# Transposes of an attention step in one block, scores two steps ahead, v in shared 8-row units

## Chip, core and metric

The kernel runs on one core of a Trainium2 chip. The metric is the time of one execution in device microseconds; the median of three executions stands for a kernel. All loads, the matmuls, the softmax and the stores are in that time. Engines are named as in the profile: PE (matmul; PEld its weight loads), DVE, ACT, POOL, and SP, which here issues the DMA transfers.

## What is computed

An encoder layer over two sequences, a prompt of 256 tokens and a sample of 2048 tokens, width 1024. Tokens stand on a grid of 64 columns: 4 rows for the prompt, 32 for the sample. One half of the inner width (8 heads of 64) is neighbourhood attention: a query sees 8 rows by 16 columns of keys. The other half is a Fourier mix. The part that matters here, from the reference:

```
def one_row(r):
    rs = jnp.clip(r - kr // 2, 0, rows - kr)
    ...
    k_slab = lax.dynamic_slice_in_dim(kg, rs, kr, axis=1)[:, :, slab_cols]
    v_slab = lax.dynamic_slice_in_dim(vg, rs, kr, axis=1)[:, :, slab_cols]
    logits = jnp.einsum('bjqhd,bijkhd->bhjqik', q_blk, k_slab).astype(jnp.float32) * scale
    ...
    logits = jnp.where(valid[:, :, None, :], logits + bias, NEG_INF)
    p = jax.nn.softmax(logits.reshape(shp[:4] + (kr * K_SLAB_COLS,)), axis=-1).reshape(shp)
    out = jnp.einsum('bhjqik,bijkhd->bjqhd', p.astype(v.dtype), v_slab)
...
mixed = jnp.concatenate([rms_norm(y_a, g_na) * jax.nn.silu(z_a),
                         rms_norm(y_f, g_f) * jax.nn.silu(z_f)], axis=-1)
out = mixed @ w_out
return x + rms_norm(out, g_post)
```

## The kernel before

The program has three stages: the input projections (to about 540 us), the Fourier mix (to 611 us), then attention together with the Fourier half of the output projection (611 to 855 us), and last the attention half of the output projection.

**Groups and steps.** Attention works through 36 groups `G`: 4 pairs of heads `pr`, and 9 groups `i` for each. Group `i` = 0 is the prompt (`R` None). The others are a set of rows `R` = 0 to 3 and a half `hc` of the columns; `HALF[R]` names the first of two runs of 4 query rows. Runs are the partitions 0 to 63 and 64 to 127 of a tile ("halves" `y`). A group has two column blocks `b` (widths `w` of 24 or 32 key columns) and two heads `h`. For `R` over 0 the two halves see 11 key rows each, starting 4 rows apart; for `R` = 0 it is 8 rows each.

**One step** of the loop over `k` (from line 1549) does `scores` of `G[k]`, transposes and second matmul of the group before, `G[k-1]`, and one half of a tile of the Fourier output projection. PE's order is written out by hand and is the order of the program:

- `scores(G[k])` (L1169): 64x64 matmuls into four PSUM banks, two passes for each f32 matmul. `bias_max` (L1191, DVE) adds the bias table and takes the row maximum, `exps` (L1196, ACT) exponentiates with a sum, `soft` (L1200 DVE reciprocal, L1203 POOL) divides.
- `transp(f, 0)` (L1470): transposes of the weights `w` of block 0, 64 rows each; half 0 goes to bank `ptb[0]`, half 1 to `ptb[1]`. ACT copies the one, DVE the other, to `pt` (L1473).
- `f_mm(k, range(6))` (L1413): the first 6 of 12 matmuls of 128x128 with 512 columns into a bank with tag "b".
- `transp(f, 1)`: the same for block 1, into the same two banks.
- `f_mm(k, range(6, 12))`, then `f_evac(k)`: DVE (even `k`, L1445) or ACT (odd `k`, L1442) takes the bank out.
- `pv(f)` (L1486): weights times v into the one bank with tag "c"; DVE multiplies by the gate `za` (L1506), ACT squares it (L1512, or L1508 for `pr` = 0), POOL adds the squares up (L1513).

A few steps also hold `f_norm` or `a_norm` (L1450, L1457: sums of squares by matmuls of one column), `ys_mul` and `ys_split` (the inputs of later `f_mm`), and in steps 2 to 7 the squares `YSQ` (L1601, L1602). After the loop come the attention tiles `a_mm`.

**PSUM** has eight banks: three "a" and two "b", two "t" (`ptb`), one "c". Three of the four score banks of a step come from "a" and the fourth from "b".

**v.** `prep_v` (L1134) loads for each group its own 4 chunks of 4 key rows for both blocks, in 4 DMAs; 3 buffers, issued at the end of step `k` for `G[k+1]`. Chunks start at row `4R'` of half 0; half 1 stands in the score tile with its key rows rotated (`ORD`), so that two of its three chunks lie at the same place as those of half 0. `pv` thus has four products per block and head: two for both halves (128 columns), one for each half alone (64 columns).

Of the kernel before, what the change touches and what calls it, by code (L numbers as in the profile page):

```python
# [178 lines left out]
def build(tc, A, O):  # L179
# [934 lines left out]


    def prep_v(g):
        cs = slice(g["pr"] * 128, g["pr"] * 128 + 128)
        v = g["v"] = jl.tile([128, 8, 128], F32, tag="v", name="v", bufs=VB)
        g["za"] = jl.tile([128, 256], F32, tag="za", name="za", bufs=VB)
        g["ch"], g["pp"] = [], []  # L1120
        if g["R"] is None:
            nc.sync.dma_start(v[:, :4], vP.rearrange("k r c e -> (r c) k e")[:, :, cs])
            nc.sync.dma_start(g["za"], zD[1, cs, :TP])
            for b in range(2):
                g["ch"].append([(0, 128)])
                g["pp"].append([(0, x, 128, 2 * b + x, True, True) for x in range(2)])
            return
        r0, r1 = HALF[g["R"]]
        for b, w in enumerate(g["kw"]):
            n = 4 * w  # L1130
            src = vD[2 * g["hc"] + b]
            parts = ((0, 3, r0 - 4), (3, 1, r1 + 3)) if g["R"] else ((0, 2, 0), (2, 2, 24))
            for j, m, r in parts:
                nc.sync.dma_start(v[:n, 4 * b + j:4 * b + j + m],  # L1134
                                  src[r:r + 4 * m].rearrange("r c e -> (r c) e")[:, cs]
                                  .rearrange("(j p) e -> p j e", p=n))
            if g["R"]:
                g["ch"].append([(0, n), (n, n), (2 * n, 3 * w)])
                g["pp"].append([(1, None, n, 4 * b + 1, True, False), (2, None, 3 * w, 4 * b + 2, False, False),
                                (0, 0, n, 4 * b, False, False), (0, 1, n, 4 * b + 3, False, True)])  # L1140
            else:
                g["ch"].append([(0, n), (n, n)])
                g["pp"].append([(j, x, n, 4 * b + 2 * x + j, j == 0, j == 1) for x in range(2) for j in range(2)])
        for x, n, r in halves(g):
            t0 = TP + 1024 * (r // 16) + 512 * g["hc"] + 32 * (r % 16)
            nc.sync.dma_start(g["za"][:, x:x + n], zD[1, cs, t0:t0 + n])


    def scores(g):
        nr = g["nr"]  # L1150
        kk = KK[g["pr"]].rearrange("p (r c) -> p r c", c=64)
        if "w" in g:
            sp = [ps.tile([128, 352], F32, tag="c", name="s", bufs=1), *ptb,
                  ps.tile([128, 352], F32, tag="a", name="s", bufs=3)]
        else:
            sp = [ps.tile([128, 352], F32, tag="b" if x == 3 else "a", name="s", bufs=2 if x == 3 else 3)
                  for x in range(4)]
        R = g["R"]
        for b, w in enumerate(g["kw"]):
            if R is None:  # L1160
                seq = [(y, 0, 4, 0, KP0[2 * b + y]) for y in range(2)]
            else:
                c0, r = KC0[2 * g["hc"] + b], 4 + HALF[R][0] - 4 * (R > 0)
                seq = [(0, r, 11, 0, c0), (1, r + 11, 4, 0, c0), (1, r + 4, 7, 4, c0)] if R else \
                    [(y, r + 24 * y, 8, 0, c0) for y in range(2)]
            for y, k, n, j, c0 in seq:
                for h in range(2):
                    hs = slice(64 * h, 64 * h + 64)
                    nc.tensor.matmul(sp[2 * b + h][64 * y:64 * y + 64, j * w:(j + n) * w],  # L1169
                                     g["q"][hs, 128 * b + 64 * y:128 * b + 64 * y + 64],  # L1170
                                     kk[hs, k:k + n, c0:c0 + w], start=True, stop=True)
# [250 lines left out]

    def f_mm(k, js=range(12)):
        d, n = ftiles[k // 2], k % 2
        if js[0] == 0:
            d["p"] = ps.tile([128, 512], F32, tag="b", name="po", bufs=2)
        out_mm(d, n, js, d["p"], lambda n, x, c: wo1[n][c][:, x])

    def a_mm(d, n, js=range(12)):
        if js[0] == 0:  # L1430
            d["p"] = ps.tile([128, 512], F32, tag="a" if n else "b", name="po", bufs=3 if n else 2)
        out_mm(d, n, js, d["p"], lambda n, x, c: WO[x][:, c, n * 512:n * 512 + 512])

# [13 lines left out]
    def f_norm(ts):  # L1447
        p = ps.tile([128, 18], F32, tag="c", name="pfn", bufs=1)
        for t in ts:
# [4 lines left out]
    def a_norm(ds):  # L1454
        p = ps.tile([128, 128], F32, tag="c", name="pna", bufs=1)
        for j, d in enumerate(ds):
# [3 lines left out]

    def transp(g, b):
        ch = g["ch"][b]
        n, z = len(ch) * 128, ch[0][1]
        o = jp.tile([128, 2, 384], F32, tag="pt", name="pt", bufs=PB)
        m = len(ch)
        for h in range(2):
            for j, (c0, nk) in enumerate(ch):
                for y in range(2):
                    ys, x = slice(64 * y, 64 * y + 64), 64 * (h * m + j)
                    nc.tensor.transpose(ptb[y][:nk, x:x + 64], g["w"][b][ys, h, c0:c0 + nk], ident[ys, ys])  # L1470
        ov = o.rearrange("p h (j y x) -> p y h j x", y=2, x=64)
        for y, copy in ((0, nc.scalar.copy), (1, V.tensor_copy)):
            copy(ov[:z, y, :, :m], ptb[y][:z, :n].rearrange("p (h j x) -> p h j x", h=2, x=64))  # L1473
        g["pt"] = g.get("pt", []) + [o]

    yt = {}

    def pv(g):
        pr, R = g["pr"], g["R"]
        p = ps.tile([128, 2, 128], F32, tag="c", name="pv", bufs=1)  # L1480
        for b, pp in enumerate(g["pp"]):
            for j, y, nk, v, first, last in pp:
                o = slice(0, 128) if y is None else slice(64 * y, 64 * y + 64)
                for h in range(2):
                    hs = slice(64 * h, 64 * h + 64)
                    nc.tensor.matmul(p[hs, b, o], g["v"][:nk, v, hs], g["pt"][b][:nk, h, j * 128 + o.start:j * 128 + o.stop],  # L1486
                                     start=first, stop=last)
# [44 lines left out]
    f_mm(0)  # L1532
    transp(G[0], 0)
    f_norm(range(2))
    transp(G[0], 1)
    ys_mul(ftiles[1])
    soft(G[1], 1)
    run_later()
# [3 lines left out]
    f_evac(1)  # L1542
    pv(G[0])
    ys_load(ftiles[2])
    prep_v(G[2])
    prep(G[4])
    for k in range(2, len(G) + 1):
        pr, i = divmod(k, 9)
        g, f = G[k] if k < len(G) else None, G[k - 1] if k else None
        if pr < 3:  # L1550
# [11 lines left out]
        if 24 <= k < 32:  # L1562
            y = k - 24
            nc.sync.dma_start(WO[y % 2][:, y // 2].bitcast(F32), woD[0, y % 2, y // 2])
        x = k // 2 + 1
        if g:
            scores(g)
            if 2 < k < 34 and k % 2 == 0:
                ys_mul(ftiles[x])
                if x + 1 < 18:  # L1570
                    ys_load(ftiles[x + 1])
            bias_max(g, 0, 0)
            exps(g, 0, 0)
            bias_max(g, 0, 1)
            bias_max(g, 1, 0)
        if f:
            transp(f, 0)
        if g:
            exps(g, 0, 1)
            bias_max(g, 1, 1)  # L1580
            exps(g, 1, 0)
            f_mm(k, range(6))
            soft(g, 0)
            exps(g, 1, 1)
            if k in NT:
                f_norm(NT[k])
            if k in (32, 34):
                a_norm(atiles[:6] if k == 32 else atiles[6:10])
# [5 lines left out]
        if g:  # L1594
            soft(g, 1)
            if k == 2:
                ys_mul(ftiles[x])
                ys_load(ftiles[x + 1])
# [4 lines left out]
        if g:  # L1603
            f_mm(k, range(6, 12))
        else:
            a_mm(atiles[0], 0, range(6, 12))
        if pr < 3 and i == 8:
            mask_p(pr + 1)
# [12 lines left out]
        if k + 3 < len(G):  # L1621
            prep(G[k + 3])
        if k == 28:
# [21 lines left out]
    def a_evac(d, n):  # L1645
        if n == 0:
            d["sa"] = sm.tile([128, 6], F32, tag="sa", name="sa")
        evac(d, d.pop("p"), slice(n * 512, n * 512 + 512), n)

# [52 lines left out]
    for j, d in enumerate(atiles):  # L1702
# [25 lines left out]
        a_mm(d, 1)  # L1728
        a_evac(d, 1)
# [20 lines left out]
```

## Time and profile before

| | |
|---|---|
| three executions | 960.94, 959.48, 960.78 us; median 960.78 |
| the profiled execution | 960.85 us, its span 959.1 us (1.75 us lie around the span) |
| PE busy, 618 to 848 us (the step loop) | 228.09 of 230.00 us |
| DVE, ACT, POOL busy there | 140.34, 137.40, 118.33 us |
| DMA share there | 0.89 at 266 GB/s |

How it is read: a busy PE only says that a matmul is under way; matmuls overlap, and a block of them that starts late because the array had to empty still counts as busy. So the time of a block is taken from its start to the start of the next block, in the timeline. In a timeline row stand the start and the duration in us, engine, line, operation, tile written and tiles read, shape, the count, and in brackets the idle time before it with its releaser. "64*96 64x64" is 64 rows by 96 columns of weights with 64 rows by 64 columns streamed past.

### The profile page before, as it was taken

What the parts mean: (1) busy time and instruction counts of PE and PEld (TensorE: products, weight loads), DVE (VectorE), ACT (ScalarE), POOL (GpSimd) and SP (SyncE); (2) the same over time, 40 slices, a digit from 0 to 9 for tenths busy, and PEclk for the clock granted to TensorE, in tenths of its full rate; (3) what the DMA queues carried; (4) which work ended last, traced back from release to release, by engine and by line L of the source; (5) the groups of instructions that cost most, each with busy time, mean ns of one, the idle gap of its engine ahead of it and who ended that gap; (6) DMA issues with size and microseconds to landing.
All of it is one profiled execution on the core that took longest, in us unless ns stands there. A gap on an engine that the chain in (4) does not pass through costs nothing.

```text
span 959.1 us, 18563 instructions
## 1 busy us (share of the span) xinstructions
PE 947.5 (99%) x6608; PEld 780.6 (81%) x6608; DVE 667.1 (70%) x1303; ACT 468.7 (49%) x1035; POOL 339.8 (35%) x338
## 2 busy tenths in 40 slices
PE   9999999999999999999999999999999999999996
PEld 7889988888888888888888888877777776888885
DVE  6387978777866976776767354676655655559997
ACT  6846676523333632223444144666555655644443
POOL 3101202445730401533433000554456554424444
PEclk9999999999999999999999999999999999999998
DMA  9899686558746998489989788598898899899993
GB/s 335 320 378 363 206 310 242 171 215 294 276 191 256 368 411 315 178 271 318 324 281 322 262 304 319 206 255 249 266 279 270 242 282 295 256 325 336 335 347 116
DMA packets 158363, 270.67 MB, mean 282 GB/s; under 512 B 22656, under 2 KB 98304, under 8 KB 155392
## 3 DMA queue, kind: packets, MB, share of 16 engines
q1 hardware_dynamic: 158128, 269.50, 81.4%
q8 instruction: 52, 0.85, 0.3%
q14 instruction: 39, 0.32, 0.1%
q10 hardware_dynamic: 144, 0.00, 0.0%
HBM read 180.91 MB, written 95.88 MB: 289 GB/s over the span
## 4 chain that ended last, share of the span: by engine, by line
PE 96%; DMA 2%; DVE 1%; ACT 1%; issue 0%; DVEq 0%; SPq 0%; ACTq 0%
PE po L1413 21%; PE mm L175 18%; PE mm L176 18%; PE mm L174 18%; PE pv L1486 5%; PE s L1169 4%; PE ptb L1470 3%; PE pab L1014 2%; PE py L174 1%; PE py L176 1%; PE py L175 1%; DMA oD<-ofs 1%; DMA rv<-wv 0%; PE ppq L1051 0%; PE pz L175 0%
## 5 line engine op out<-in xcount | busy, mean ns | idle before, releaser
L174 PE MATMUL mm<-xh,wa 128*128 128x512 f32 x448 | 174.4, 389 | 0.0
L175 PE MATMUL mm<-xl,wa 128*128 128x512 f32 x448 | 174.3, 389 | 0.0
L176 PE MATMUL mm<-xh,wa 128*128 128x512 f32 x448 | 174.3, 389 | 0.0
L176 PEld LDWEIGHTS mm<-xh,wa 128*128 128x128 f32 x448 | 84.1, 188 | 17.5
L174 PEld LDWEIGHTS mm<-xh,wa 128*128 128x128 f32 x448 | 84.1, 188 | 17.5
L175 PEld LDWEIGHTS mm<-xl,wa 128*128 128x128 f32 x448 | 84.1, 188 | 17.2
L1203 POOL TENSOR_SCALAR w<-w,m 128x352 f32<-128x352 f32 (+4 forms) x136 | 75.3, 567 | 55.9 <-DVE m L1200 49.7
L1413 PE MATMUL po<-wo,yh 128*128 128x512 f32 x272 | 92.0, 419 | 0.0
L551 POOL TENSOR_TENSOR ws<-wr 128x512 f32<-128x512 f32 x16 | 21.5, 1341 | 185.1 <-DMA wr<-wz 128.2
L1413 PE MATMUL po<-w,yh 128*128 128x512 f32 x280 | 86.8, 391 | 0.0
L566 DVE TENSOR_TENSOR wa<-wr,wa 128x512 fp32r<-128x512 f32 x60 | 57.1, 959 | 33.2 <-ACT wa L565 32.9
L1196 ACT ACTIVATE w<-w,m 128x352 f32<-128x352 f32 (+4 forms) x136 | 70.2, 519 | 13.2 <-DVE m L1191 12.9
L868 DVE TENSOR_TENSOR f<-u,mm 128x512 f32<-128x512 f32 x64 | 43.6, 681 | 33.6 <-PE mm L176 28.8
L175 PE MATMUL mm<-vl,xh 128*128 128x512 f32 x168 | 65.5, 390 | 0.2 <-DVE vl L497 0.2
L176 PE MATMUL mm<-vh,xl 128*128 128x512 f32 x168 | 65.4, 389 | 0.0
L174 PE MATMUL mm<-vh,xh 128*128 128x512 f32 x168 | 65.4, 389 | 0.0
L1413 PEld LDWEIGHTS po<-w,yh 128*128 128x128 f32 x280 | 52.3, 188 | 10.8
L1191 DVE CUSTOM_DVE_ANT_1 w<-s,tb 128x264 f32<-128x264 f32 (+3 forms) x124 | 51.8, 454 | 11.1 <-PE s L1169 10.3
L565 ACT CAST wa<-wr 128x512 fp32r<-128x512 f32 x60 | 36.3, 617 | 45.0 <-PE mm L176 17.6
L1486 PEld LDWEIGHTS pv<-pt,v 96*64 96x64 f32 (+2 forms) x1088 | 45.0, 137 | 14.7 <-issue 11.7
L1413 PEld LDWEIGHTS po<-wo,yh 128*128 128x128 f32 x272 | 45.8, 188 | 11.4
L1413 PE MATMUL po<-w,yl 128*128 128x512 f32 x140 | 54.5, 389 | 0.0
(245 smaller groups left out, 2187.1 us busy)
## 6 DMA issues: line engine op xcount, KB each, us to landing
wr<-wz SPq DMA_DIRECT2D x48, 512.0 KB
vl<-sD SPq DMA_DIRECT2D x20, 512.0 KB
xm<-xm SPq DMA_DIRECT2D x9, 1024.0 KB
oD<-ofs SPq DMA_DIRECT2D x18, 512.0 KB
of<-oD SPq DMA_DIRECT2D x18, 512.0 KB
yr<-yD SPq DMA_DIRECT2D x34, 256.0 KB
zD<-f SPq DMA_DIRECT2D x16, 512.0 KB
woD<-wo SPq DMA_DIRECT2D x16, 512.0 KB
```

The source lines that it names most:

```text
L174: nc.tensor.matmul(out, lh, rh, start=first, stop=False)
L175: nc.tensor.matmul(out, lh, rl, start=False, stop=False)
L176: nc.tensor.matmul(out, ll, rh, start=False, stop=last)
L565: nc.scalar.copy(o[:, 0], src)
L566: nc.vector.tensor_tensor(out=o[:, 1], in0=src, in1=o[:, 0].bitcast(F32), op=ALU.subtract)
L868: nc.vector.tensor_tensor(out=dst(f, b), in0=src(uu[u]), in1=src(p), op=op)
L1169: nc.tensor.matmul(sp[2 * b + h][64 * y:64 * y + 64, j * w:(j + n) * w], g["q"][hs, 128 * b + 64 * y:128 * b + 64 * y + 64], kk[hs, k:k + ...
L1191: nc.vector.tensor_tensor_reduce(out=rows(g["w"][b][:, h, :n], w), in0=rows(g["s"][2 * b + h][:, :n], w), in1=tv, scale=1.0, scalar=3.0e38 ...
L1196: nc.scalar.activation(w, w, AF.Exp, bias=m[:, h:h + 1], scale=-1.0, accum_out=m[:, 2 + h:3 + h])
L1203: nc.gpsimd.tensor_scalar(w, w, m[:, 4 + h:5 + h], 1.0, ALU.mult, ALU.mult)
L1413: nc.tensor.matmul(p, (d["l"] if x == 2 else d["h"])[:, c], w(n, int(x == 1), c), start=j == 0, stop=j == 11)
L1486: nc.tensor.matmul(p[hs, b, o], g["v"][:nk, v, hs], g["pt"][b][:nk, h, j * 128 + o.start:j * 128 + o.stop], start=first, stop=last)
```

## The change

The transposes of both blocks of a group now run as one block of `transp(g)` into four banks, and `f_mm` as one block of 12. The group transposed and multiplied in step `k` is `G[k-2]`; the loop has one step more. The order on PE becomes transposes, scores, `f_mm`, (norms), `pv`. The two "b" banks become `ptb[2]` and `ptb[3]`: block 1's transposes write there first, and later in the same step `f_mm(k)` writes into one of them, `ptb[2 + k % 2]`. The fourth score bank is now "c", the bank of `pv`; the norms use "a". `f_mm(0)` and `f_mm(1)` write `ptb[0]` and `ptb[1]`; the first transposes follow them directly. The two halves of the first attention tile run in steps 36 and 37.

v is loaded in units of 8 key rows (2 chunks), one for each group after the first two units; a unit serves the group that loads it and the next one of the same columns. 6 buffers of half the size take the place of 3. Both halves' chunks of a group now lie at the same rows of a unit only for the middle chunk, so `pv` has five products per block and head, one of 128 columns and four of 64. In `scores` half 1 is rotated by 8 rows in place of 7: pieces of 3 and 8 rows in place of 4 and 7. Query tiles are loaded one step earlier, `mask_p` runs one step earlier.

```diff
-ORD = ((0, 1, 2, 3, 4, 5, 6, 7, 8, 9, 10), (7, 8, 9, 10, 0, 1, 2, 3, 4, 5, 6))
+ORD = ((0, 1, 2, 3, 4, 5, 6, 7, 8, 9, 10), (8, 9, 10, 0, 1, 2, 3, 4, 5, 6, 7))
...
-VB = 3
+VB = 6
+ZB = 4
...
+    def unit(g, u):
+        v = VU[g["hc"], u] = jl.tile([128, 2, 2, 128], F32, tag="v", name="v", bufs=VB)
+        for b, w in enumerate(g["kw"]):
+            n = 4 * w
+            nc.sync.dma_start(v[:n, b], vD[2 * g["hc"] + b][8 * u:8 * u + 8, :, g["pr"] * 128:g["pr"] * 128 + 128]
+                              .rearrange("(j r) c e -> (r c) j e", j=2))
...
+        for u in (3, 0) if R == 0 else (R,):
+            unit(g, u)
...
+                A, B = VU[g["hc"], R - 1], VU[g["hc"], R]
+                g["ch"].append([((0, n), (0, m)), ((n, n), (m, n)), ((2 * n, m), (m + n, n))])
+                g["pp"].append([(1, None, n, A, 1, True, False), (2, 0, m, B, 0, False, False),
+                                (2, 1, n, B, 0, False, False), (0, 0, n, A, 0, False, False),
+                                (0, 1, m, B, 1, False, True)])
...
-            sp = [ps.tile([128, 352], F32, tag="b" if x == 3 else "a", name="s", bufs=2 if x == 3 else 3)
+            sp = [ps.tile([128, 352], F32, tag="c" if x == 3 else "a", name="s", bufs=1 if x == 3 else 3)
...
-                seq = [(0, r, 11, 0, c0), (1, r + 11, 4, 0, c0), (1, r + 4, 7, 4, c0)] if R else \
+                seq = [(0, r, 11, 0, c0), (1, r + 12, 3, 0, c0), (1, r + 4, 8, 3, c0)] if R else \
...
+    def bank(k):
+        return ptb[k if k < 2 else 2 + k % 2]
...
+    def transp(g):
+        g["pt"] = []
+        for b, ch in enumerate(g["ch"]):
+            m = len(ch)
+            z = ch[0][0][1]
+            o = jp.tile([128, 2, 384], F32, tag="pt", name="pt", bufs=PB)
+            for j, c in enumerate(ch):
+                for h in range(2):
+                    for y, (c0, nk) in enumerate(c):
+                        ys, x = slice(64 * y, 64 * y + 64), 64 * (h * m + j)
+                        nc.tensor.transpose(ptb[2 * b + y][:nk, x:x + 64], g["w"][b][ys, h, c0:c0 + nk], ident[ys, ys])
+            ov = o.rearrange("p h (j y x) -> p y h j x", y=2, x=64)
+            for y, copy in ((0, nc.scalar.copy), (1, V.tensor_copy)):
+                copy(ov[:z, y, :, :m], ptb[2 * b + y][:z, :128 * m].rearrange("p (h j x) -> p h j x", h=2, x=64))
...
     f_mm(0)
-    transp(G[0], 0)
     f_norm(range(2))
-    transp(G[0], 1)
...
-    pv(G[0])
...
-    for k in range(2, len(G) + 1):
+    for k in range(2, len(G) + 2):
...
+        transp(f)
+        if p:
+            soft(p, 1)
         if g:
             scores(g)
...
             bias_max(g, 0, 0)
             exps(g, 0, 0)
             bias_max(g, 0, 1)
+            exps(g, 0, 1)
             bias_max(g, 1, 0)
-        if f:
-            transp(f, 0)
...
-            f_mm(k, range(6))
             soft(g, 0)
             exps(g, 1, 1)
...
+            f_mm(k)
         else:
-            a_mm(atiles[0], 0, range(6))
-            a_norm(atiles[10:14])
-        if f:
-            transp(f, 1)
...
+            a_mm(atiles[0], k - 36)
...
-        if g:
-            f_mm(k, range(6, 12))
...
-        if f:
-            pv(f)
+        pv(f)
```

More of the change, by code (lines that the diff above doesn't have):

```diff
@@ L1117, in prep_v @@
         cs = slice(g["pr"] * 128, g["pr"] * 128 + 128)
-        v = g["v"] = jl.tile([128, 8, 128], F32, tag="v", name="v", bufs=VB)
-        g["za"] = jl.tile([128, 256], F32, tag="za", name="za", bufs=VB)
-        g["ch"], g["pp"] = [], []
[L1121 to L1140, printed above, removed]
-            else:
-                g["ch"].append([(0, n), (n, n)])
-                g["pp"].append([(j, x, n, 4 * b + 2 * x + j, j == 0, j == 1) for x in range(2) for j in range(2)])
+        R = g["R"]
@@ new lines, in prep_v @@
+        za = g["za"] = jl.tile([128, 256], F32, tag="za", name="za", bufs=ZB)
+        if R is None:
+            v = jl.tile([128, 2, 2, 128], F32, tag="v", name="v", bufs=VB)
+            nc.sync.dma_start(v.rearrange("p b x e -> p (b x) e"), vP.rearrange("k r c e -> (r c) k e")[:, :, cs])
+            nc.sync.dma_start(za, zD[1, cs, :TP])
+            g["ch"] = [[((0, 128),) * 2]] * 2
+            g["pp"] = [(0, x, 128, v, x, True, True) for x in range(2)]
+            g["pp"] = [g["pp"]] * 2
+            return
@@ new lines, in prep_v @@
+        for u in (3, 0) if R == 0 else (R,):
+            unit(g, u)
+        g["ch"], g["pp"] = [], []
+        for w in g["kw"]:
+            n, m = 4 * w, 3 * w
+            if R:
+                A, B = VU[g["hc"], R - 1], VU[g["hc"], R]
[3 more added lines that the diff above has]
+                                (0, 1, m, B, 1, False, True)])
+            else:
+                g["ch"].append([((0, n),) * 2, ((n, n),) * 2])
+                g["pp"].append([(j, x, n, VU[g["hc"], 3 * x], j, j == 0, j == 1) for x in range(2) for j in range(2)])
@@ L1421, in xt_load, with f_mm, a_mm @@
         nc.sync.dma_start(d["xt"], A["xn"][d["t"] * 128:d["t"] * 128 + 128, :])
-    def f_mm(k, js=range(12)):
+    def bank(k):
+        return ptb[k if k < 2 else 2 + k % 2]
+    def f_mm(k):
         d, n = ftiles[k // 2], k % 2
[L1425 to L1432, printed above, removed]
+        d["p"] = bank(k)
+        out_mm(d, n, range(12), d["p"], lambda n, x, c: wo1[n][c][:, x])
+    def a_mm(d, n):
+        x = n or d is atiles[0]
+        p = ps.tile([128, 512], F32, tag="a" if x else "b", name="po", bufs=3 if x else 2)
+        d["p", n] = p
+        out_mm(d, n, range(12), p, lambda n, x, c: WO[x][:, c, n * 512:n * 512 + 512])
     def f_evac(k):
@@ L1447, in f_norm @@
     def f_norm(ts):
-        p = ps.tile([128, 18], F32, tag="c", name="pfn", bufs=1)
+        p = ps.tile([128, 18], F32, tag="a", name="pfn", bufs=3)
         for t in ts:
@@ L1454, in a_norm @@
     def a_norm(ds):
-        p = ps.tile([128, 128], F32, tag="c", name="pna", bufs=1)
+        p = ps.tile([128, 128], F32, tag="a", name="pna", bufs=3)
         for j, d in enumerate(ds):
@@ L1459, in a_norm @@
         rsq_ops(inva[:, ds[0]["i"]:ds[0]["i"] + n], p[:, :n], n, 1.0 / 512)
[L1461 to L1474, printed above, removed]
+    def transp(g):
[12 more added lines that the diff above has]
+                copy(ov[:z, y, :, :m], ptb[2 * b + y][:z, :128 * m].rearrange("p (h j x) -> p h j x", h=2, x=64))
+            g["pt"].append(o)
     yt = {}
@@ L1481, in pv @@
         for b, pp in enumerate(g["pp"]):
-            for j, y, nk, v, first, last in pp:
+            for j, y, nk, v, x, first, last in pp:
                 o = slice(0, 128) if y is None else slice(64 * y, 64 * y + 64)
@@ L1485, in pv @@
                     hs = slice(64 * h, 64 * h + 64)
-                    nc.tensor.matmul(p[hs, b, o], g["v"][:nk, v, hs], g["pt"][b][:nk, h, j * 128 + o.start:j * 128 + o.stop],
+                    nc.tensor.matmul(p[hs, b, o], v[:nk, b, x, hs], g["pt"][b][:nk, h, j * 128 + o.start:j * 128 + o.stop],
                                      start=first, stop=last)
@@ L1532, in build @@
     f_mm(0)
-    transp(G[0], 0)
     f_norm(range(2))
-    transp(G[0], 1)
     ys_mul(ftiles[1])
-    soft(G[1], 1)
+    ptb += [ps.tile([128, 512], F32, tag="b", name="ptb", bufs=2) for x in range(2)]
+    for x in range(2, 4):
+        V.memset(ptb[x], 0.0)
     run_later()
@@ L1546, in build @@
     prep(G[4])
-    for k in range(2, len(G) + 1):
+    prep(G[5])
+    for k in range(2, len(G) + 2):
         pr, i = divmod(k, 9)
-        g, f = G[k] if k < len(G) else None, G[k - 1] if k else None
+        g, p, f = G[k] if k < len(G) else None, G[k - 1] if k <= len(G) else None, G[k - 2]
         if pr < 3:
@@ L1565, in build @@
         x = k // 2 + 1
+        transp(f)
+        if p:
+            soft(p, 1)
         if g:
             scores(g)
-            if 2 < k < 34 and k % 2 == 0:
+            if k < 34 and k % 2 == 0:
                 ys_mul(ftiles[x])
@@ L1574, in build @@
             bias_max(g, 0, 1)
+            exps(g, 0, 1)
             bias_max(g, 1, 0)
-        if f:
-            transp(f, 0)
-        if g:
-            exps(g, 0, 1)
+            exps(g, 1, 0)
             bias_max(g, 1, 1)
-            exps(g, 1, 0)
-            f_mm(k, range(6))
             soft(g, 0)
             exps(g, 1, 1)
[L1585 to L1588, printed above, removed]
-        else:
-            a_mm(atiles[0], 0, range(6))
-            a_norm(atiles[10:14])
-        if f:
-            transp(f, 1)
[L1594 to L1598, printed above, removed]
+            f_mm(k)
+        else:
+            a_mm(atiles[0], k - 36)
+        if k in NT:
+            f_norm(NT[k])
+        if k in (32, 34, 36):
+            a_norm(atiles[{32: slice(6), 34: slice(6, 10), 36: slice(10, 14)}[k]])
         run_later()
@@ L1602, in build @@
             V.tensor_tensor(out=sqs[:, x0:x1], in0=sqs[:, x0:x1], in1=v[:, x0:x1], op=ALU.add)
-        if g:
-            f_mm(k, range(6, 12))
-        else:
-            a_mm(atiles[0], 0, range(6, 12))
-        if pr < 3 and i == 8:
+        if pr < 3 and i == 7:
             mask_p(pr + 1)
@@ L1620, in build @@
             prep_v(G[k + 1])
-        if k + 3 < len(G):
-            prep(G[k + 3])
+        if k + 4 < len(G):
+            prep(G[k + 4])
         if k == 28:
@@ L1647, in a_evac @@
             d["sa"] = sm.tile([128, 6], F32, tag="sa", name="sa")
-        evac(d, d.pop("p"), slice(n * 512, n * 512 + 512), n)
+        evac(d, d.pop(("p", n)), slice(n * 512, n * 512 + 512), n)
     def part_sum(sa):
@@ L1727, in build @@
                 residual(atiles[j - 1], n)
-        a_mm(d, 1)
+            a_mm(d, 1)
         a_evac(d, 1)
```

3 lines of the change are left out of this document (2 added, 1 removed).

## The prediction

> **What bounds the kernel.** First I read the busy shares of the page and its chain that ended last, then the waits of PE.
>
> ```profile
> PE 947.5 (99%) x6608; PEld 780.6 (81%) x6608; DVE 667.1 (70%) x1303; ACT 468.7 (49%) x1035; POOL 339.8 (35%) x338
> PE 96%; DMA 2%; DVE 1%; ACT 1%; issue 0%; DVEq 0%; SPq 0%; ACTq 0%
> PE pv L1486 <- DMA v<-vD: 1.6, 1, 1.6
> PE s L1169 <- DMA q<-qD: 0.2, 1, 0.2
> ```
>
> PE is busy 99% of the span and makes up 96% of the chain; in the whole step loop it waits for anything visible once for v and once for q. No other engine can be relieved to any profit: only what PE does, or how densely it does it, counts. So the next view is PE's timeline, one ordinary step (`R` over 0), read from start to start.
>
> ```profile
> 705.76 1.28 PE L1169 MATMUL s<-kk,q 64*64 64x352 f32 x24
> 706.97 0.54 PE L1470 MATMUL ptb<-ident,w 64*96 64x64 f32 x12
> 707.44 0.74 PE L1413 MATMUL po<-wo,yh 128*128 128x512 f32 x2
> 708.02 0.40 PE L1413 MATMUL po<-wo,yl 128*128 128x512 f32 x1
> 708.25 0.63 PE L1413 MATMUL po<-wo,yh 128*128 128x512 f32 x2
> 708.72 0.39 PE L1413 MATMUL po<-wo,yl 128*128 128x512 f32 x1
> 709.04 0.58 PE L1470 MATMUL ptb<-ident,w 64*128 64x64 f32 x12
> 709.54 0.73 PE L1413 MATMUL po<-wo,yh 128*128 128x512 f32 x2
> ...
> 711.13 1.57 PE L1486 MATMUL pv<-pt,v 96*64 96x128 f32 x32
> 712.63 1.28 PE L1169 MATMUL s<-kk,q 64*64 64x264 f32 x24
> ```
>
> The step lasts 712.63 - 705.76 = 6.87 us and has six blocks, each of another tile shape than its neighbours. Within a block of `f_mm` three matmuls take 708.72 - 708.02 = 0.70, so 0.233 each and 1.40 for six; the block takes 709.04 - 707.44 = 1.60. So 0.20 us goes at its two ends. Where the shape does not change, no such gap shows:
>
> ```profile
> 610.99 0.34 PE L176 MATMUL py<-abh,pql 128*128 128x384 f32 x1
> 611.18 2.92 PE L1413 MATMUL po<-wo,y0h 128*128 128x512 f32 x12
> ```
>
> Here `f_mm(0)` follows matmuls of its own shape 0.19 us after the last of them. The ends cost because the array changes its shape, and the change has fewer of them.
>
> **Transposes in one block.** Blocks of 4, 8 and 12 transposes of 128 columns give the fixed part.
>
> ```profile
> 733.51 0.34 PE L1470 MATMUL ptb<-ident,w 64*128 64x64 f32 x4
> 733.77 0.73 PE L1413 MATMUL po<-wo,yh 128*128 128x512 f32 x2
> ...
> 740.70 0.46 PE L1470 MATMUL ptb<-ident,w 64*128 64x64 f32 x8
> 741.10 0.73 PE L1413 MATMUL po<-wo,yh 128*128 128x512 f32 x2
> ...
> 742.68 1.15 PE L1486 MATMUL pv<-pt,v 96*64 96x64 f32 x32
> 743.77 1.28 PE L1169 MATMUL s<-kk,q 64*64 64x264 f32 x24
> ```
>
> 4 take 0.26, 8 take 0.40, 12 take 709.54 - 709.04 = 0.50: four more cost 0.12, and 0.14 is fixed. The count of transposes is the same after the change, and the stream past each is 64 columns as now. 72 blocks (two per group) become 36: 36 x 0.14 = **5.0 us gained**. The new neighbours, `pv` before and `scores` behind, change shape as the old ones do.
>
> **f_mm in one block.** One block of 12 between transposes and `pv` stands in the trace, `f_mm(1)`:
>
> ```profile
> 615.10 3.02 PE L1413 MATMUL po<-wo,y0h 128*128 128x512 f32 x12
> 618.05 0.69 PE L1486 MATMUL pv<-pt,v 128*64 128x64 f32 x16
> 618.67 0.99 PE L1169 MATMUL s<-kk,q 64*64 64x256 f32 x16
> 619.59 0.43 PE L1470 MATMUL ptb<-ident,sc 64*96 64x64 f32 x8
> ```
>
> It takes 2.95; two blocks of six take 1.60 + 1.59 = 3.19. 0.24 a step for 35 steps (2 to 36): **8.4 us gained**. At the end `pv` now stands between the two halves of the first attention tile, one more block end: 2.95 - 12 x 0.233 = **0.15 lost**.
>
> **pv with five products.** The 16 instructions of the prompt (64 columns) take 0.62, the 32 of `R` = 0 (64 columns) 1.09: 16 narrow ones cost 0.47, and 0.15 is fixed. The ordinary 32 (half narrow, half wide) take 1.50, so 16 wide ones cost 0.88. New: 8 wide and 32 narrow, 0.44 + 0.94 + 0.15 = 1.53. **0.03 x 24 groups = 0.7 lost.** If a narrow one among unequal row counts cost as much as a wide one (0.055), it would be 10 us; the rows of narrow ones are at hand, so I take 0.7.
>
> **scores.** Both rotations stream 11 key rows per half, so I cost it at 0. Block `R` = 0 takes 0.92 for 448 columns per quarter of the array and the step's 616 columns take 1.21: a piece of 32 columns that sticks out would be 0.06, so at most 1.4 us either way.
>
> **v and its wait.** The one visible wait is dearer than its 1.6 us.
>
> ```profile
> 800.46 0.40 PE L1413 MATMUL po<-wo,yl 128*128 128x512 f32 x1
> 802.46 1.59 PE L1486 MATMUL pv<-pt,v 96*64 96x64 f32 x32 [1.60 <-DMA v<-vD]
> 804.28 2.33 PE L1169 MATMUL s<-kk,q 64*64 64x264 f32 x24 [0.24 <-DMA q<-qD]
> 806.54 0.68 PE L1470 MATMUL ptb<-ident,w 64*128 64x64 f32 x8
> ...
> 805.00:810.00 5.00, 5.00 (x44) 3.49 (x38) 2.83 (x12) 2.93 (x10) 1.62 (x2) 0.79 0.89 248
> ```
>
> The last row is a stretch of 5 us behind the wait; the third number from its end is the granted clock, 0.79. Undisturbed, `pv` would start 0.32 after the last `f_mm` (as 709.04 after 708.72), and the transposes 1.09 + 1.21 later, at 803.08. They start at 806.54: 3.46 us, of which 1.84 is waiting and 1.6 a lower clock behind it. After the change v is asked for at the end of the same step but needed a step (6.5 us) later, q a step earlier, and a group loads 2 chunks where it loaded 4. **3.5 us gained.** If some DMA wait stays, the gain goes to 0.
>
> **Waits that come in.** They are on banks. Block 1's transposes need both "b" banks, so `f_evac` of the step before; the fourth score bank needs `pv` of the step before taken out; `f_mm` needs block 1's copy (ACT's in even steps, DVE's in odd ones). Step 36 of the present kernel has transposes straight behind `pv`, so its rows show how soon the copies come.
>
> ```profile
> 848.08 0.58 PE L1470 MATMUL ptb<-ident,w 64*128 64x64 f32 x12
> ...
> 848.20 0.42 DVE L1506 TENSOR_TENSOR y<-pv,za 128x256 f32<-128x256 f32 x1 [2.43 <-PE pv L1486]
> 848.72 0.56 DVE L1473 COPY pt<-ptb 128x384 f32<-128x384 f32 x1
> ...
> 848.71 0.38 ACT L1512 ACTIVATE sqa<-pv 128x256 f32<-128x256 f32 x1 [1.33 <-DVE y L1506]
> 848.99 0.47 ACT L1473 COPY pt<-ptb 128x384 f32<-128x384 f32 x1
> ```
>
> From the start of the transposes (848.08): ACT squares from 0.63 to 1.01, copies block 0 from 0.91; block 1's copy follows 0.47 later at most and ends at 1.85. DVE copies from 0.64, ends block 1 at 0.64 + 2 x 0.56 = 1.76. The new transposes take 0.47 + 0.50 - 0.14 = 0.83 and the scores 1.21, so `f_mm` is due at 2.04: ordinary steps have 0.2 to 0.3 to spare. The fourth score bank, free at 1.0, is due at 0.83 + 0.6 = 1.4. `f_evac` (0.69 to 0.75) has the 1.5 us of `pv` and 0.5 us of block 0 as cover. Queued behind a late copy are `bias_max` on DVE and `exps` on ACT, which have the 2.95 us of `f_mm` before anyone needs them; POOL's division has a whole step more than now.
>
> The cover is thinner in four places.
>
> ```profile
> 618.16 0.69 ACT L1442 ACTIVATE ofs<-po,invf 128x512 f32<-128x512 f32 x1 [2.00 <-PE po L1413]
> 726.34 0.67 PE L1169 MATMUL s<-kk,q 64*64 64x128 f32 x16
> 726.94 0.57 PE L1470 MATMUL ptb<-ident,w 64*128 64x64 f32 x12
> ```
>
> (a) The first transposes need `ptb[1]` right behind `f_mm(1)`, and `pv`, which covered the 0.69 of its copy-out, is gone: 618.16 + 0.69 - 618.05, and an estimated 0.1 to hand over, 0.9 us lost. (b) Steps with the prompt's scores (9, 18, 27) have 0.60 in place of 1.21: `f_mm` is due at 1.43 and waits 0.3 to 0.4 us, 1.0 in all. (c) Behind the prompt's short transposes (11, 20, 29) the fourth score bank is due at about 0.9: 0.1 each; with (b) I take 1.2 us, of 0 to 4. (d) Steps 2 and 3 put `YSQ` squares ahead of `f_evac` with a short `pv` as cover; from `f_evac`'s 0.75 a step I take 1.5 us, of 0 to 3.
>
> **Sum.** -5.0 - 8.4 - 3.5 + 0.15 + 0.7 + 0.9 + 1.2 + 1.5 = -12.5 us. The profiled execution took 960.85 us, 0.07 over the median shown: 960.85 - 12.5 = **948.4 us**.
>
> **Rivals.**
>
> *The banks bind in every even step.* If hand-overs take 0.3 us longer than the rows of step 36, each even step waits some 0.3 us for ACT's copy: 17 x 0.3 = 5 us, 953.5. For it: the margin is only 0.2. Against it: the rows are of just this order of work.
>
> *Short waits pull the clock down.* 1.84 us of waiting cost 1.6 more behind it at 800 us. If the waits of (a) to (d), of 0.3 to 1 us in some seven places, did the same, 7 x 1.4 = 10 us come back: 958. Against it: they are a fifth to a half as long.
>
> The Trainium skill, "TensorE: Matmul & The Clock Gate", in its section "Why this matters for your kernels", asks only that no idle gap exceed about 3 us. The trace differs: a gap of 1.6 us was followed by 0.79. By the page's rule this rival would cost nothing.
>
> *The stretch without full-array matmuls gets too long (slower).* From the end of one `f_mm` to the next run now `pv`, scores and 12 transposes, 1.50 + 1.21 + 0.47 = 3.18 us, at a clock of 1.00:
>
> ```profile
> 705.76:712.63 6.87, 6.87 (x97) 5.28 (x93) 4.06 (x14) 4.58 (x13) 3.26 (x5) 1.00 0.88 256
> ```
>
> After the change it is 1.53 + 0.83 + 1.21 = 3.57. If such work counted as rest, with a limit between 3.18 and 3.57, each of 34 steps would lose something like the 1.6 us at 800 us: 54 us, about 1003. It takes 0.37 us a step (12.5 / 34) to turn the result into a loss. Against it: nothing in the loop's 3.18 dents the clock, and two thirds of the stretch are plain matmuls.
>
> "TensorE: Matmul & The Clock Gate" in the Trainium skill says in "Part 4: PE-mode transpose" that transposes do not count as busy in the same way. No row here shows that; by it the stretch would be the 0.83 of transposes alone.
>
> *The block ends stay.* If the 0.14 and 0.24 belonged to something else than the change of shape, such as the wait for copies, only v's 3.5 us would come, against 4.4 of losses: 961.8, no difference. Against it: the row at 611.18.
>
> **Chances.** Forecast 0.75 (945 to 951.5, from no added waits to double); banks in every step 0.13 (951.5 to 956); short waits and the clock 0.04 (955 to 960); ends stay 0.04; slower 0.04. Range 945.0 to 954.0: it holds the forecast and half or more of the second case, some 0.82. 0.2% (1.9 us) is about what a measurement of this kernel can tell from no change; faster 0.91, same 0.04, slower 0.05 (the slower case and a part of the ends that stay).
>
> **What would show it.** Right: ordinary steps of about 6.5 us in place of 6.87, with four blocks; 24 transposes in 0.83, 12 `f_mm` in 2.95, `pv` in 1.53; no wait of PE for v; clock 1.00 through the loop; small waits of PE for ACT or DVE at the start of the loop and at the prompt's steps only. Wrong: PE waiting for ACT's copies in most steps, a clock under 1.00 in the loop, `pv` blocks over 1.6, or a new wait for v, q or the gate.

## The result and the profile after

| | before | after |
|---|---|---|
| median, with lowest and highest of four executions | 960.65 us (959.48 to 960.94) | 952.86 us (952.14 to 954.12) |
| ratio, with its 95% interval | | 0.9923 [0.9905, 0.994] |
| the profiled execution, its span | 960.85, 959.1 us | 952.14, 950.3 us |

The change made the kernel 7.8 us faster. The forecast was 948.4 us in a range of 945.0 to 954.0. The profiled execution of after is the fastest of its four, so the sums below, made from traces, stand some 0.7 us under the median.

The busy shares and the chain that ended last, from the page of after:

```profile
PE 936.1 (99%) x6800; PEld 780.1 (82%) x6800; DVE 663.7 (70%) x1305; ACT 467.3 (49%) x1035; POOL 332.5 (35%) x338
...
PE 93%; DVE 2%; DMA 2%; issue 1%; ACT 1%; SPq 0%; DVEq 0%; ACTq 0%
```

PE still sets the end. It works 11.4 us less than before, yet the span is only 8.8 us shorter, and the chain now holds 2% of DVE. The view of PE's waits in the step loop of after names them (waiting engine, tile and line, what released it; sum, times, longest):

```profile
PE ptb L1482 <- DVE ofs L1456: 3.3, 6, 1.3
PE ptb L1482 <- ACT ofs L1453: 0.4, 1, 0.4
PE ptb L1421 <- ACT pt L1485: 0.3, 1, 0.3
PE ptb L1421 <- DVE pt L1485: 0.2, 1, 0.2
```

The wait for v has gone. New is the first row: transposes that wait for `f_evac`'s copy on DVE, because they write a bank that `f_mm` has used. Two of its six waits stand at the start of the loop (0.17 and 0.61 us), where the prediction has its places (a) and (d); the other four (0.16, 0.47, 0.56 and 1.28 us) stand each in the step behind a norm, where the prediction has none. An ordinary step shows none of this (PE's timeline of after):

```profile
642.98 1.59 PE L1498 MATMUL pv<-pt,v 96*64 96x128 f32 x40
644.51 0.91 PE L1482 MATMUL ptb<-ident,w 64*128 64x64 f32 x24
645.35 1.28 PE L1177 MATMUL s<-kk,q 64*64 64x352 f32 x24
646.55 0.73 PE L1421 MATMUL ptb<-wo,yh 128*128 128x512 f32 x2
...
649.50 1.59 PE L1498 MATMUL pv<-pt,v 128*64 128x128 f32 x40
```

From start to start: `pv` 1.53, transposes 0.84, scores 1.20, `f_mm` 649.50 - 646.55 = 2.95. Together 6.52 us, with four blocks, where the step took 6.87.

Adding every block of the loop in this way (from the first `f_mm` to the end of the last `pv`; in the kernel before on to the end of the first attention tile, whose second half stands behind the last `pv` there) gives where the time went, but for rounding:

| us | before | after | difference |
|---|---|---|---|
| transposes, without waits and slow clock | 31.6 | 26.6 | -5.0 |
| `f_mm`, without the wait for v | 119.2 | 111.7 | -7.5 |
| `pv`, without slow clock | 47.4 | 47.7 | +0.2 |
| scores, without waits and slow clock | 37.2 | 37.2 | 0 |
| norms | 7.1 | 6.9 | -0.2 |
| wait for v and q, slow clock behind it | 3.6 | 0 | -3.6 |
| waits of transposes and scores | 0 | 6.6 | +6.6 |
| the loop | 246.2 | 236.8 | -9.4 |

A wait is here what a block lasts longer than an undisturbed one of its kind; that counts hand-overs which the view of waits, at 4.2 us, leaves out. One wait stands in another row: `f_mm(1)` lasts 3.20 us in place of 2.95, because the first transposes behind it wait. The loop starts 0.44 us later than before and the work behind it is 0.15 us longer, which makes the 8.8 us of the span.

The largest wait, in the step after `f_norm` at `k` = 4 (timeline of after, PE, ACT and DVE):

```profile
634.99 0.50 PE L1461 MATMUL pfn<-ones,sqs 128*128 128x1 f32 x4
...
635.53 0.26 ACT L1367 ACTIVATE dl<-pfn,epst 128x2 f32<-128x2 f32 x1 [0.90 <-PE pfn L1461]
...
635.83 0.16 DVE L1369 TENSOR_SCALAR ds<-pfn 128x2 f32<-128x2 f32 x1 [2.00 <-ACT dl L1367]
...
636.45 0.16 DVE L1374 SCALAR_TENSOR_TENSOR invf<-dt,dy 128x2 f32<-128x2 f32 x1
...
636.69 0.83 DVE L1606 TENSOR_TENSOR sqs<-sqs,Y 128x640 f32<-128x640 f32 x1
637.43 0.75 DVE L1456 TENSOR_SCALAR ofs<-ptb,invf 128x512 f32<-128x512 f32 x1
...
638.33 0.57 PE L1482 MATMUL ptb<-ident,w 64*128 64x64 f32 x12 [1.28 <-DVE ofs L1456]
```

`f_mm(4)` is done when the norm's matmuls start, at 634.99. Its copy-out starts 2.44 us later: in DVE's order, which is the program's, the norm's chain stands in front of it (which waits for ACT's Ln, and that for PE), then the squares of `YSQ`. `pv` and block 0 of the transposes, which should have covered the copy, are over by then. The six steps behind a norm (norms at `k` = 4, 8, 10, 12, 32, 34) lose 3.66 us in this way, counted by blocks; after `k` = 8 and 32 the loss, 0.27 and 0.12 us, does not show in the view of waits.

### The profile page after: what moved, and what is told of

Read it like the earlier page. It is cut to its first block, busy times and chain, and to the rows that moved or that the text cites. A ratio compares the mean times of both kernels' runs of the same rounds, so it can differ in the third digit from the quotient of the medians.

```text
span 950.3 us, 18824 instructions
## 1 busy us (share of the span) xinstructions
PE 936.1 (99%) x6800; PEld 780.1 (82%) x6800; DVE 663.7 (70%) x1305; ACT 467.3 (49%) x1035; POOL 332.5 (35%) x338
## 4 chain that ended last, share of the span: by engine, by line
PE 93%; DVE 2%; DMA 2%; issue 1%; ACT 1%; SPq 0%; DVEq 0%; ACTq 0%
PE mm L176 18%; PE mm L177 18%; PE mm L175 18%; PE ptb L1421 10%; PE po L1421 10%; PE pv L1498 4%; PE s L1177 4%; PE ptb L1482 3%; PE pab L1015 2%; PE py L175 1%; PE py L177 1%; PE py L176 1%; DMA za<-zD 1%; DVE ofs L1456 0%; DMA rv<-wv 0%
## 5 line engine op out<-in xcount | busy, mean ns | idle before, releaser
L1421 PE MATMUL ptb<-wo,yh 128*128 128x512 f32 x272 | 88.2, 405 | 0.5 <-ACT pt L1485 0.3
L1211 POOL TENSOR_SCALAR w<-w,m 128x352 f32<-128x352 f32 (+4 forms) x136 | 65.9, 499 | 46.6 <-DVE m L1208 26.2
L1421 PEld LDWEIGHTS ptb<-wo,yh 128*128 128x128 f32 x272 | 48.4, 188 | 20.2 <-ACT pt L1485 5.6
L1421 PE MATMUL ptb<-wo,yl 128*128 128x512 f32 x136 | 53.2, 391 | 0.0
```

The costliest lines, as they stand in the source:

```text
L1211: nc.gpsimd.tensor_scalar(w, w, m[:, 4 + h:5 + h], 1.0, ALU.mult, ALU.mult)
L1421: nc.tensor.matmul(p, (d["l"] if x == 2 else d["h"])[:, c], w(n, int(x == 1), c), start=j == 0, stop=j == 11)
```

## The experiments

Each ratio is to the kernel before, run beside it on the same chip. The kernel before had a median of 960.81 us beside `e1_norms` to `e4_all`, 961.88 beside `e5_order` to `e7_lead` and 960.82 beside `e8_split`. No kernel leaves work out.

**Do the norms cause the loss in the six steps?** `e1_norms` puts `f_norm` ahead of `f_mm`, and `f_evac` ahead of the squares or of `a_norm`:

```diff
+            if k in NT:
+                f_norm(NT[k])
             f_mm(k)
...
-        if k in NT:
-            f_norm(NT[k])
+        if k in (32, 34):
+            f_evac(k)
...
         run_later()
+        if k in NT:
+            f_evac(k)
```

> The changed kernel with one thing moved: in steps 4, 8, 10 and 12 the norm's matmuls stand ahead of the twelve f_mm matmuls, and in these steps and in 32 and 34 the copy-out of the f_mm bank stands ahead of the second half of the norm's vector work that it does not need. Theory A (the missing 3 to 4 us are the transposes of block 1 in steps 5, 9, 11, 13, 33 and 35, which wait for a copy-out queued behind the norm): in the trace of the change these six transposes last 3.7 us more than their kind, so 952.9 becomes about 949.2, ratio to the kernel before 0.988, and their blocks last 0.40, 0.62 or 0.83. Theory B (another engine is the bound by now, and a wait removed comes back at the next bank): 952 to 953, ratio 0.991 to 0.992.

Measured: 950.53 us (949.16 to 951.55), ratio 0.9894 [0.9876, 0.9911]; the span of the profiled execution is 949.5 us. The transposes take 28.1 us where after has 31.9, and in the six steps they last as long as undisturbed ones; the two waits at the start of the loop are still there. The scores take 1.3 us more. PE's timeline shows the place at `k` = 4, and the view of PE's waits names it:

```profile
631.98 1.44 PE L1177 MATMUL s<-kk,q 64*64 64x352 f32 x24
633.57 0.61 PE L1461 MATMUL pfn<-ones,sqs 128*128 128x1 f32 x4 [0.16 <-DVE m L1199]
```
```profile
PE pfn L1461 <- DVE m L1199: 0.7, 3, 0.3
```

Scores to norm take 1.59 in place of 1.20: the norm, now straight behind the scores, needs an "a" bank, and DVE's row maximum still reads it. So the loss is the norms', as the theory said, and a third of what is won goes into the next bank. The time came out between the two theories.

**Which part brings what?** `e2_v_only` is the kernel before with the units of v, five products and the new rotation; `e3_blocks_only` is the kernel after with the 4-row chunks, four products and old rotation.

```diff
-VB = 3
+VB = 6
+ZB = 4
...
+        for u in (3, 0) if R == 0 else (R,):
+            unit(g, u)
```
```diff
-VB = 6
+VB = 3
...
-        for u in (3, 0) if R == 0 else (R,):
-            unit(g, u)
...
+            parts = ((0, 3, r0 - 4), (3, 1, r1 + 3)) if g["R"] else ((0, 2, 0), (2, 2, 24))
```

> The kernel before with the v part alone: units of 8 rows, five products, 6 buffers, scores rotated by 8; order of blocks, lag and banks as before. Theory A: the wait for v at 800 us and the slow clock behind it go (3.5 us), five products cost 0.5 to 0.7: 957.5 to 958.2, ratio 0.997. Theory B: the wait was one of many chances for v to be late and another takes its place: 960.5 to 962, ratio 1.000 to 1.001.

> The changed kernel with v as before: each group loads its four chunks, four products, 3 buffers, rotation by 7; blocks, lag and banks as changed. Theory A (the lag alone gives v the time, the units only save traffic): the wait for v is gone, pv is 0.02 us shorter in 24 groups, so 952 to 952.6, ratio 0.991. Theory B (units are needed, the DMA share of 0.9 does not carry the shorter step): waits for v come back, 954.5 to 957, ratio 0.994 to 0.996.

Measured: v alone 957.32 us (956.61 to 959.29), 0.9965 [0.9954, 0.9977]; blocks alone 961.48 us (959.49 to 966.21), 1.0011 [0.9998, 1.0024]. The parts do not add: -3.5 and +0.7 us apart, -7.8 us together. The trace of `e3_blocks_only` is of the slowest of its twelve executions (966.21 us), so it shows where the loss lies, and more of it than the median has. First its waits of 780 to 845 us, then two rows of PE's timeline there:

```profile
POOL yr L1391 <- DMA yz<-zD: 26.6, 4, 8.4
ACT sqa L1517 <- DVE y L1511: 19.3, 8, 7.5
...
DVE y L1511 <- DMA v<-vD: 5.8, 1, 5.8
```
```profile
807.59 0.77 PE L1491 MATMUL pv<-pt,v 128*64 128x64 f32 x16 [0.96 <-DMA v<-vD]
...
813.49 1.15 PE L1170 MATMUL s<-kk,q 64*64 64x264 f32 x10 [3.33 <-ACT sqa L1517]
```

Loads are late there: v for PE and DVE, the gate `yz` for POOL. Behind a late `y` ACT's squares are late, and the bank that they read is the fourth score bank, for which PE stands 3.33 us. The theory that a group's two steps of delay suffice for v falls; its rival was right in kind, and too small.

The row of 780 to 845 us in the view by stretches (busy time of PE, PEld, DVE, ACT, POOL, then granted clock, DMA share, GB/s), for before, after and `e3_blocks_only`:

```profile
780.00:845.00 65.00, 63.13 (x792) 48.02 (x790) 37.26 (x140) 36.46 (x118) 32.25 (x52) 0.97 0.93 281
```
```profile
780.00:845.00 65.00, 64.26 (x908) 52.10 (x899) 36.30 (x143) 37.36 (x121) 29.87 (x53) 1.00 0.89 274
```
```profile
780.00:845.00 65.00, 55.38 (x684) 43.43 (x680) 32.53 (x122) 31.49 (x101) 27.61 (x47) 0.95 0.93 278
```

With 4-row chunks the DMA moves some 280 GB/s at a share of 0.93 with either order of PE. That left two theories: that the units win because they are asked for earlier, or because they are fewer bytes.

**Lead or bytes?** `e6_traffic` is after with an additional 8-row load for each group with `R` over 0, into a tile that nobody reads. `e7_lead` is after with v, its gate included, asked for one step later.

```diff
+        if R:
+            w2 = jl.tile([128, 2, 2, 128], F32, tag="v2", name="v2", bufs=1)
+            for b, w in enumerate(g["kw"]):
+                nc.sync.dma_start(w2[:4 * w, b], vD[2 * g["hc"] + b][8 * R - 8:8 * R, :, cs]
+                                  .rearrange("(j r) c e -> (r c) j e", j=2))
```
```diff
-        if k + 1 < len(G):
-            prep_v(G[k + 1])
+        if 2 < k < len(G):
+            prep_v(G[k])
```

> The changed kernel, with one more unit of v loaded in each group of R over 0 into a tile that nobody reads: the transfers of v are again as many bytes as before the change, with the new buffers, the new lead and five products. Theory C (the blocks need the bytes that the units save): late transfers as in the run of the blocks alone, 957 to 962. Theory D (the blocks alone failed by three buffers, whose loads are issued only behind pv of the same step): 952.5 to 954.

> The changed kernel with v and the gate asked for one step later: bytes as changed, lead as in the kernel before. Theory C (bytes decide): 952.5 to 954.5. Theory D (the lead decides): waits for v or the gate come back, 956 to 961.

Measured: `e6_traffic` 962.04 us (958.59 to 964.6), 1.0002 [0.9981, 1.0024]; `e7_lead` 953.15 us (950.97 to 954.75), 0.9912 [0.989, 0.9934]. The later request costs nothing that can be told from noise, and PE waits for no v in it. The unread loads take the whole gain away. The sums of all transfers stand on the pages, first after's, then `e6_traffic`'s:

```profile
DMA packets 146846, 265.20 MB, mean 279 GB/s; under 512 B 21889, under 2 KB 86785, under 8 KB 143873
```
```profile
DMA packets 158365, 270.71 MB, mean 282 GB/s; under 512 B 22656, under 2 KB 98304, under 8 KB 155392
```

The kernel before has 270.67 MB in 158363 packets, so this is its traffic under the new order of PE. The waits of 780 to 845 us are those of `e3_blocks_only` again, though v has all of after's lead:

```profile
ACT sqa L1529 <- DVE y L1523: 20.3, 9, 7.2
POOL yr L1403 <- DMA yz<-zD: 20.0, 4, 8.1
...
DVE y L1523 <- DMA v<-vD: 5.8, 1, 5.8
```

Up to 768 us `e6_traffic` keeps pace with after (156.2 us from the first `f_mm` in both), so the loss lies behind that. The transfers are thus the next bound, close behind PE: at the old traffic the shorter PE work ends where it did before, and 5.5 MB less make room for it. Bytes, packets and the DMA issues that go with them were not separated, so it is not shown that the 16 DMA engines are what is full. A rival is the queue of SP, which issues one transfer after the other. Its longest wait before an issue between 700 and 845 us is 5.6 us in after (first row), but 1.5 us in `e3_blocks_only` (second row) and 1.2 us in `e6_traffic`: there SP goes from issue to issue. In such a row stand the sum of the waits, how many they are, and the longest.

```profile
SPq L1454 <- ACT ofs L1453: 15.3, 6, 5.6
```
```profile
SPq L1109 <- DMA tb<-tD: 1.5, 1, 1.5
```

**Can the waits be had back?** `e4_all` is `e1_norms` with two more edits: `f_evac` ahead of the `YSQ` squares in every even step, and `f_mm` of steps 9, 18 and 27 in a bank that comes free earlier.

```diff
-        return ptb[k if k < 2 else 2 + k % 2]
+        return ptb[k % 2 if k < 2 or k % 9 == 0 else 2 + k % 2]
...
+        if g and k % 2 == 0 and k not in (32, 34):
+            f_evac(k)
         for v, x0, x1 in YSQ.get(k, []):
```

> As the run with the norms moved, and the copy-out ahead of the YSQ squares in all even steps, and f_mm of steps 9, 18 and 27 in a bank of block 0, whose copy comes first. Theory A (every added wait is such a queue order): 0.8 us of step 3 and 0.7 us of steps 9, 18 and 27 go as well: about 947.7, ratio 0.9865. Theory B: no better than the run with the norms alone.

Measured: 950.73 us (949.86 to 952.46), 0.9897 [0.9879, 0.9915], no better than `e1_norms`. The waits at steps 9, 18 and 27 have gone. Another came at step 3, as DVE's part of the timeline and a row of PE's waits show:

```profile
624.35 0.75 DVE L1456 TENSOR_SCALAR ofs<-ptb,invf 128x512 f32<-128x512 f32 x1 [1.49 <-PE ptb L1421]
625.01 2.09 DVE L1610 TENSOR_TENSOR sqs<-sqs,Y 128x256 f32<-128x256 f32 x2
627.03 0.47 DVE L1518 TENSOR_TENSOR y<-pv,za 128x128 f32<-128x128 f32 x2
```
```profile
PE s L1177 <- ACT ysq L1520: 1.2, 1, 1.2
```

DVE stands 1.49 us for the end of `f_mm`, copies out, and only then does the squares, which last 2.09 us here and 1.21 in after, for a reason not looked into. Behind all of it comes `y`, which empties the bank of `pv`, the fourth score bank. `e5_order` keeps the norm ahead of `f_mm` only at `k` = 4 and 8, puts just `f_evac` ahead of the norm at 10, 12, 32 and 34, keeps the bank of steps 9, 18 and 27, and spreads the squares over steps 2 to 9:

```diff
+            if k in (4, 8):
+                f_norm(NT[k])
             f_mm(k)
...
-        if k in NT:
+        if k in (10, 12, 32, 34):
+            f_evac(k)
+        if k in (10, 12):
             f_norm(NT[k])
...
-    YSQ = {2: [(Y2, 256, 512), (Y2, 512, 1024)], 3: [(Y, 256, 512), (Y2, 1024, 1664)], 4: [(Y2, 1664, 2304)],
-           5: [(Y, 512, 1110)], 6: [(Y, 1110, 1708)], 7: [(Y, 1708, 2304)]}
+    YSQ = {2: [(Y2, 256, 512)], 3: [(Y, 256, 512)], 4: [(Y2, 512, 1024)], 5: [(Y2, 1024, 1664)],
+           6: [(Y2, 1664, 2304)], 7: [(Y, 512, 1110)], 8: [(Y, 1110, 1708)], 9: [(Y, 1708, 2304)]}
```

> The changed kernel with only orders moved: norms ahead of f_mm in steps 4 and 8 alone, where the copy-out needs them; in 10, 12, 32 and 34 the copy-out ahead of the norm; f_mm of steps 9, 18 and 27 in a bank of block 0; the YSQ squares spread over steps 2 to 9, one in each, in place of two in steps 2 and 3. Theory A (the added waits are queue orders, and what came back in the two runs before came from the norm's own bank in steps 10 and 12 and from the doubled squares in 2 and 3): of the 6.6 us of added waits in the trace of the change some 4 to 4.5 go, 948.5, ratio 0.9875. Theory B (what is taken away at one bank comes back at the next): 950.5 to 951, ratio 0.9895 as those two.

Measured: 948.54 us (947.64 to 948.76), 0.9864 [0.9847, 0.988]. That is below both kernels; its interval does not touch after's. PE's waits in the step loop:

```profile
PE pfn L1461 <- DVE m L1199: 0.6, 2, 0.3
PE ptb L1482 <- ACT ofs L1453: 0.4, 1, 0.4
PE ptb L1482 <- DVE ofs L1456: 0.2, 1, 0.2
```

Counted by blocks, 2.3 us of added waits are left of after's 6.6; `f_mm` and `pv` take 111.8 and 47.7 us, as in after.

**Are the block ends real?** `e8_split` is `e5_order` with `f_mm` in two blocks of six and the first block of `pv` between them. The same instructions are issued, in six blocks a step (`pv(f, 0)` does block 0, the `pv(f)` at the end of the step block 1):

```diff
-            f_mm(k)
+            f_mm(k, range(6))
+            pv(f, 0)
+            f_mm(k, range(6, 12))
```

> The kernel with the orders moved, and in steps 2 to 35 six f_mm matmuls, pv of block 0, the other six, pv of block 1: the same matmuls, two more blocks a step, no new operand to wait for. Theory A (a block's ends cost because the array changes its shape: 0.23 us for f_mm in two blocks, 0.15 for pv in two): 34 x 0.38 = 13 us more, 961.4, ratio about 1.000; in the trace of this run two blocks of six last about 3.2 together and pv about 1.65 in place of 1.52. Rival (the ends were waits for data and left with the waits): 948.5 to 950, ratio 0.986 to 0.988.

Measured: 963.88 us (962.71 to 964.98), 1.0032 [1.0017, 1.0046], 15.3 us over `e5_order` by the medians and 16.0 by the spans of the traces (961.8 and 945.8 us). One step of its PE timeline:

```profile
709.59 0.73 PE L1421 MATMUL ptb<-wo,yh 128*128 128x512 f32 x2
...
711.22 0.91 PE L1502 MATMUL pv<-pt,v 128*64 128x128 f32 x20
712.05 0.73 PE L1421 MATMUL ptb<-wo,yh 128*128 128x512 f32 x2
...
713.64 0.91 PE L1502 MATMUL pv<-pt,v 96*64 96x128 f32 x20
714.47 0.90 PE L1482 MATMUL ptb<-ident,w 64*96 64x64 f32 x24
```

`f_mm` takes 1.63 + 1.59 and `pv` 0.83 + 0.83, without a wait in any row. Over the loop `f_mm` grows by 7.87 us and `pv` by 5.23, which is 0.23 and 0.15 for each of the 34 additional ends of either kind. Together they are the 13 us that were expected. Another 2.5 us are longer blocks of transposes and scores, whose cause was not looked into. The rival, that the ends were waits for data, falls.

## Why the prediction was right or wrong

- **The step and its blocks: right.** Steps of 6.5 us with four blocks were forecast, 6.52 came. The transposes saved 5.0 of 5.0 us. `f_mm` saved 7.5 of 8.25 (8.4 less the 0.15 at the end): 0.22 a step, where I had read 0.24 off one step, and 0.25 of what is missing is the wait behind `f_mm(1)`. Five products in `pv` cost 0.25 us in the table and about 0.65 by the medians of one block (1.523 us for 1.496, in 24 groups), of the 0.7; the difference is three blocks of 1.6 to 1.7 us in before, whose cause stays open. The scores cost nothing, as taken.
- **v's wait: right in size, too narrow in meaning.** 3.5 us forecast, 3.6 in the trace, and v alone, five products included, gave 3.5 in the medians. But I took the terms for v and for the blocks as independent. "If some DMA wait stays, the gain goes to 0" was said of the 3.5 us only. In fact the blocks' 12.5 us, some 6 after the waits that come with them, hang on the units: blocks alone ended at 1.0011. The row that I had quoted for the ordinary step, with its DMA share of 0.88, would have led to the question of how much shorter PE's work could get before the transfers end last. The forecast was not hurt, since both parts came together.
- **The waits that I listed: there, and a little smaller.** (a) 0.85 for 0.9, of which 0.25 stands in the row of `f_mm`; (b) and (c) 1.04 for 1.2; (d) 1.04 for 1.5.
- **The step that failed** is the sentence "`f_evac` (0.69 to 0.75) has the 1.5 us of `pv` and 0.5 us of block 0 as cover". It holds in ordinary steps. In the six with a norm, DVE has the norm's chain to do ahead of `f_evac`, and the chain cannot start before PE's norm, which stands behind all twelve `f_mm`. I looked at what covers the copy and not at what is queued in front of it. That is 3.66 us at 0 in the sum. `e1_norms` took these waits away. Of the prediction's signs of being right one did not hold: "small waits of PE for ACT or DVE at the start of the loop and at the prompt's steps only".
- **Start of the loop:** 0.44 us later than before, not forecast and not looked into.

So the gap of 3.7 us between the forecast and the profiled execution is the norms' 3.66, 0.44 at the start and 0.75 at `f_mm` (the 0.25 of (a) with it), less about 1.1 of other terms that came out smaller, `pv` and the listed waits. With the norms' order mended, `e5_order` comes to 948.5.

The rivals: *the banks bind in every even step* gave 953.5, near the result, but by luck: its mechanism is another, and the ordinary steps wait for nothing. *Short waits pull the clock down* falls for waits of this length: behind the 1.28 us wait at 637 us the clock stays at 1.00, in the view by stretches of after:

```profile
638.00:640.00 2.00, 1.67 (x36) 1.28 (x36) 1.88 (x6) 1.13 (x3) 0.27 (x1) 1.00 1.15 312
640.00:645.00 5.00, 5.00 (x72) 4.13 (x70) 3.23 (x12) 3.94 (x11) 1.63 (x4) 1.00 0.97 256
```

After's row of 780 to 845 us above has a clock of 1.00 too, over steps with 3.57 us between two `f_mm`, so *the stretch without full-array matmuls* falls. (Of the 3.57 us 2.74 are plain matmuls, more than the two thirds that I had put.) *The block ends stay* falls by the block sums and by `e8_split`.

## What to carry to other kernels

When a copy-out moves to another place or its bank gets a new user, list for every kind of step, the rare ones too, what its engine has queued in front of it and when that can start; cover counted from the producer's side alone is not enough. When an engine busy 99% is to be relieved, ask which bound is next: here, at a DMA share of 0.9, late transfers swallowed some 6 us of net gain until the traffic shrank with it. Where PE alternates between tile shapes, look for fewer and longer blocks of one shape; here a block more or less made 0.14 us (transposes), 0.15 (`pv`) or 0.23 (`f_mm`).

## What the hardware showed beyond that

A block's end on PE has a price when the tile shape changes: 0.23 us more for each additional block of `f_mm`, 0.15 for each of `pv`, in `e8_split`. In front of a norm, whose matmuls have `f_mm`'s own 128*128 tile, a block of six takes 1.50 us in before, and 1.59 in front of another shape. The Trainium skill, "TensorEngine Tiling (Array Packing)", says under "Tiling Modes", "Key Properties", that a change of the tiling mode drains the engine. The runs agree with this, though they show only the time lost and not the drain.

The granted clock did not answer to all idle time alike. A wait of 1.28 us left it at 1.00 (above), and so did waits of 1.30 and 1.36 us in `e3_blocks_only`; 1.84 us of waiting in the kernel before, in two pieces of 1.60 and 0.24, was followed by 0.79 over 5 us; in `e3_blocks_only` the wait of 3.33 us before 813.49 us was followed by 0.55:

```profile
815.00:820.00 5.00, 5.00 (x18) 3.58 (x19) 1.49 (x6) 2.07 (x8) 2.10 (x4) 0.55 0.97 318
```

So a transfer that came late cost PE more here than the wait itself. Where between 1.36 and 1.84 us the clock begins to fall, and whether it depends on what ran before, these runs do not tell.
